# One product for two in the sums over features, and a weight remainder issued behind the norms' reciprocal

## The chip, the core and the metric

The kernel runs on one core of a Trainium2 chip. Its engines each work through a queue of their own: TensorE (PE, with its weight loads PEld), VectorE (DVE), ScalarE (ACT), GpSimd (POOL), and SyncE (SP), which issues the loads. The metric is the device time of one execution in microseconds; the kernel before takes 1084.68 us (median of 3 runs, 1083.91 to 1085.72).

## What is computed

Two layers of a hybrid decoder on 288 tokens (256 of a prompt, 32 of eight samples), 1024 features wide. Each layer has four token mixers with gates, an output product, a SwiGLU mixer and two LayerNorms; the Conformer mixer has a LayerNorm of its own over 256 channels. What the change touches are these norms:

```python
def layer_norm(x, g, b):
    xf = x.astype(jnp.float32)
    mu = jnp.mean(xf, -1, keepdims=True)
    var = jnp.mean(jnp.square(xf - mu), -1, keepdims=True)
    return ((xf - mu) * lax.rsqrt(var + LN_EPS) * g + b).astype(x.dtype)

    b_out = jax.nn.silu(layer_norm(cv + conv_b, conv_ln_g, conv_ln_b))
    ...
    x1 = layer_norm(ALPHA * x + merged @ w_o, ln1_g, ln1_b)
    ...
    r = r + (pe @ w_pe) * jax.nn.sigmoid(r @ w_pg)
    y = layer_norm(r, ln2_g, ln2_b)
```

## The kernel before

Features lie on the 128 partitions, tokens along the free axis: `xf` is 8 tiles of 128x288 in f32. Every matrix product with weights is three products of PE (L292 to L294, or L315, L321, L319 in `outer`): the rounded weight `whi` with the rounded input, `whi` with the input's remainder, and the weight's remainder `wlo` with the rounded input.

The weights come as 306 groups of 8 blocks of 128x128. `W` counts blocks; at each new group `fetch` issues what is due ahead: the load of a group (SP, `load`, tile `wraw`, 4 buffers), its rounding (ACT, `high`, L264, tile `whi`, 4 buffers) up to three groups ahead, and its remainder (DVE, `low`, L271, tile `wlo`, 3 buffers) up to two groups ahead. `fetch(g, 2)` issues only roundings that are due for group g, `fetch(g, 3)` only remainders. While `hold` is true, as in the last product ahead of a norm and in the norm itself, a new group issues loads alone.

A sum over features is a product with the constant `o1024` (every element 1/1024) in plain f32. The program writes one such instruction, and the trace shows two PE records for it.

**The two big norms of a layer** (`ln`, four calls in all). `ln_part` and `ln_square` have by then summed seven of the eight tiles: `lnt[:,1]` is the sum of tiles 4 to 6 (tiles 0 to 3 were centred earlier, in `ln_pivot`), `lnt[:,2]` is a sum of squares that POOL adds up, and `lnt[:,0]` the square of tile 7. `ln` issues the remainder that is due, then the first half of the mean product `mu` (L402), sixteen small products in quarters (`quarters`, L395) for the mean and the mean square of each token, and the second half of `mu` (L407). Then come the variance (ACT L411, DVE L412, ACT L415), a copy of `mu` to SBUF for POOL (ACT L417), one rounding (ACT L264, by `fetch(self.group - 1, 2)`), the reciprocal (DVE L419), and its spread over the partitions (PE L424, tile `rs`). After that DVE and POOL subtract the mean (L430, L432), and for each tile k, `first` multiplies with `rs` (DVE L437) and rounds with scale and offset (ACT L439, tile `xh`), `second` makes the remainder (DVE L446, L448, tile `xl`), and `after(k)` is PE's next weight product, which reads `xh` of tile k. So that PE has work meanwhile, `fill` puts small weight products with `w_pe` at three places: ahead of the sums, behind them, and behind the spread. The first norm of a layer has 4 blocks (12 products) at each of the places 1 and 2; the second norm of layer 0 has 2, 4 and 2 blocks; the last norm of all has none, and no weights are left by then. At tile 2 `fetch(self.group)` issues all that is due.

**The Conformer norm** (`conv`) is a generator that a planner steps once for each group of weights, so its instructions lie scattered among the gate products of the input projection. It sums the two tiles `cv[:,0]` and `cv[:,1]` with two products (L702), subtracts, squares on ACT (L708), and sums the two squares `sq` with two more (L712). Each `yield` of two numbers charges a cost to the planner for DVE and ACT.

Of the kernel before, what the change touches and what calls it, by code (L numbers as in the profile page):

```python
# [14 lines left out]
OP = mybir.AluOpType  # L15
# [99 lines left out]
class Builder:  # L115
# [268 lines left out]
    def ln(self, g, b, after=None, fill={}):  # L384

        nc, xf = self.nc, self.xf
        g, b = self.par(g), self.par(b)
        q = N // 4
        st, mu = self.ax(), self.ax()[:, :N]
        m4, s4 = st[:, :q], st[:, q:2 * q]  # L390
        o = self.c("o1024")

        def quarters(out, src, first=False, last=False):
            for j in range(4):
                nc.tensor.matmul(out[32 * j:32 * j + 32], o[:, :32], src[:, q * j:q * j + q], start=first, stop=last)  # L395

        d, d2, d7, d72 = self.lnt[:, 1], self.lnt[:, 2], xf[:, KD - 1], self.lnt[:, 0]
        self.fetch(self.group, 3)
        out = {}
        if 0 in fill:  # L400
            out[0] = fill[0]()
        nc.tensor.matmul(mu, o, d, start=True, stop=False)  # L402
        quarters(m4, d, first=True)
        quarters(m4, d7)
        quarters(s4, d2)
        quarters(s4, d72, last=True)
        nc.tensor.matmul(mu, o, d7, start=False, stop=True)  # L407
        if 1 in fill:
            out[1] = fill[1]()
        t = [self.sb.tile([128, q], F32, name="q", tag="q", bufs=3) for _ in range(3)]  # L410
        nc.scalar.activation(t[0], m4, AF.Square)  # L411
        nc.vector.tensor_tensor(t[1], s4, t[0], op=OP.subtract)  # L412
        if 0 in fill:
            out[0]()
        nc.scalar.activation(t[2], t[1], AF.Sqrt, bias=self.c("eps"))  # L415
        mus = self.lnt[:, 3]
        nc.scalar.activation(mus, mu, AF.Copy)  # L417
        self.fetch(self.group - 1, 2)
        nc.vector.reciprocal(t[1], t[2])  # L419
        if 1 in fill:  # L420
            out[1]()
        rs = self.ax()[:, :N]
        for j in range(4):
            nc.tensor.matmul(rs[:, q * j:q * j + q], self.c("ident")[:, 32 * j:32 * j + 1].to_broadcast([128, 128]),  # L424
                             t[1], start=True, stop=True)
        if 2 in fill:
            out[2] = fill[2]()
        nd = 2 if after else 3
        for k in range(nd):
            nc.vector.tensor_tensor(xf[:, k], xf[:, k], mu, op=OP.subtract)  # L430
        for k in range(nd, KD):
            nc.gpsimd.tensor_tensor(xf[:, k], xf[:, k], mus, op=OP.subtract)  # L432
        ys = {}

        def first(k):
            y = ys[k] = self.s()
            nc.vector.tensor_tensor(y, xf[:, k], rs, op=OP.mult)  # L437
            if after:
                nc.scalar.activation(self.xh[:, k], y, AF.Identity, bias=b[:, k:k + 1], scale=g[:, k:k + 1])  # L439

        def second(k):
            y = ys.pop(k)
            if not after and k not in (3, 7):
                nc.scalar.activation(xf[:, k], y, AF.Identity, bias=b[:, k:k + 1], scale=g[:, k:k + 1])
            else:
                nc.vector.tensor_scalar(xf[:, k], y, g[:, k:k + 1], b[:, k:k + 1], op0=OP.mult, op1=OP.add)  # L446
            if after:
                nc.vector.tensor_tensor(self.xl[:, k], xf[:, k], self.xh[:, k].bitcast(F32), op=OP.subtract)  # L448
            elif k in (0, 1, 3, 5, 6, 7):
                c = slice(k - 1 if k in (3, 5) else k, k + 1)  # L450
                nc.sync.dma_start(self.d["y"][:, c], xf[:, c])

        first(0)
        if 2 in fill:
            out[2]()
        second(0)
        first(1)
        for k in range(2, KD + 2):
            if k < KD:
                first(k)  # L460
            if k <= KD:
                second(k - 1)
            if k == 2:
                self.hold = False
                self.fetch(self.group)
            if after:
                after(k - 2)
                if k == 7:
                    self.ln_warm(AF.Sigmoid)
        self.free()  # L470
# [197 lines left out]
    def conv(self):  # L668
        nc = self.nc
        ce, w = self.ce, self.par("conv_w")  # L670
        cv = yield from self.get_b([128, 2, N])
        bias = self.par("conv_b")
        es = [ce[:, c, 30 + TP:].rearrange("p (b w) -> p b w", b=NB) for c in range(2)]
        yield VECTOR
        for j in range(31):
            for c in range(2):
                wj = w[:, 31 * c + j:31 * c + j + 1]
                o, e = cv[:, c, :TP], ce[:, c, j:j + TP]
                if j == 0:
                    nc.vector.tensor_scalar(o, e, wj, bias[:, c:c + 1], op0=OP.mult, op1=OP.add)  # L680
                else:
                    nc.vector.scalar_tensor_tensor(o, e, wj, o, op0=OP.mult, op1=OP.add)  # L682
                yield 0.49, 0
        pr = yield from self.get_b([128, NB, TS, 31])
        for c in range(2):
            e = es[c]
            e = bass.AP(tensor=e.tensor, offset=e.offset, ap=[list(e.ap[0]), [34, NB], [1, TS], [1, 31]])
            nc.vector.tensor_tensor(pr, e, w[:, None, None, 31 * c:31 * c + 31].to_broadcast([128, NB, TS, 31]),
                                    op=OP.mult)
            yield 1.1, 0  # L690
            nc.vector.tensor_reduce(bt(cv[:, c, TP:]), pr, axis=AX.X, op=OP.add)
            yield 1.1, 0
            nc.vector.tensor_scalar(cv[:, c, TP:], cv[:, c, TP:], bias[:, c:c + 1], None, op0=OP.add)
            yield 0.1, 0
        yield BOTH
        self.free()
        self.free()
        yield 1
        mu, var = yield from self.get_ax(2)
        mu, var = mu[:, :N], var[:, :N]  # L700
        for c in range(2):
            nc.tensor.matmul(mu, self.c("o1024"), cv[:, c], start=c == 0, stop=c == 1)  # L702
        sq = [self.s(), self.s()]
        for c in range(2):
            nc.vector.scalar_tensor_tensor(cv[:, c], mu, -4.0, cv[:, c], op0=OP.mult, op1=OP.add)
            yield 0.4, 0
        for c in range(2):
            nc.scalar.activation(sq[c], cv[:, c], AF.Square)  # L708
        yield 0, 0.8
        yield 1  # L710
        for c in range(2):
            nc.tensor.matmul(var, self.c("o1024"), sq[c], start=c == 0, stop=c == 1)  # L712
        sd = self.s()
        nc.scalar.activation(sd, var, AF.Sqrt, bias=self.c("eps"), scale=4.0)
        yield 0, 2.0
        yield 1
        self.free_ax(2)
        rs = self.s()
        nc.vector.reciprocal(rs, sd)
        yield 2.0, 0  # L720
        g, b = self.par("cg"), self.par("cb")
        t = [self.s(), self.s()]
        for c in range(2):
            nc.vector.tensor_tensor(cv[:, c], cv[:, c], rs, op=OP.mult)
            yield 0.4, 0
        for c in range(2):
            nc.vector.tensor_scalar(cv[:, c], cv[:, c], g[:, c:c + 1], b[:, c:c + 1], op0=OP.mult, op1=OP.add)
            yield 0.4, 0
        for c in range(2):
            nc.scalar.activation(t[c], cv[:, c], AF.Sigmoid)  # L730
            yield 0, 0.45
        yield 1
        for c in range(2):
            nc.vector.tensor_tensor(cv[:, c], cv[:, c], t[c], op=OP.mult)
            yield 0.4, 0
        self.br["conv"] = yield from self.parts(cv)
# [353 lines left out]
    def layer(self, l, outs):  # L1090
# [22 lines left out]
        self.pe_load(l)  # L1113
        self.branch(3, "attn", 4)
        self.finish(conv)
        self.drop_ax(self.tick + 1)
        assert not self.tasks and self.ax_live == 0 and self.b_live == 2 + l, (self.ax_live, self.b_live)
# [186 lines left out]
def bt(a):  # L1304
    return a.rearrange("p (b t) -> p b t", b=NB)
# [134 lines left out]
```

## Time and profile before

| | |
|---|---|
| device time, median of 3 runs | 1084.68 us |
| device time of the profiled execution | 1083.62 us |
| its span, first to last instruction | 1081.8 us |
| PE busy | 1066.2 us (99%) |
| PE weight loads busy | 1030.5 us (95%) |
| DVE busy | 770.9 us (71%) |
| ACT busy | 557.5 us (52%) |
| POOL busy | 174.4 us (16%) |
| mean granted clock of PE | 0.996 |

The profiled execution lasts 1.8 us longer than its span, and 1.1 us less than the median. PE's records overlap (a product of 288 columns has a record of 0.29 us and the next starts some 0.13 us later), so the distance of starts is what a product costs, and a stretch in which starts lie at that distance is PE-bound. A row of the timeline merges like instructions that follow each other; in square brackets stands how long the engine had been idle and what ended that.

### The profile page before, as it was taken

How to read it: one execution, taken by the hardware profiler on the slowest of the kernel's cores; microseconds unless marked ns; L12 is line 12 of the kernel's file. 1: busy time of each engine (PE TensorE's matmuls, PEld its weight loads, DVE VectorE, ACT ScalarE, POOL GpSimd, SP SyncE). 2: the span in 40 equal slices, each digit the busy share in tenths (PEclk: the TensorE clock that was granted, in tenths of full speed). 3: DMA queues.
4: the chain of work that ended last, by engine and by line, in shares of the span. 5: the costliest groups of instructions: out<-in, count | busy, mean ns of one | idle time of the engine just before them, and what ended most of it. 6: DMA issues, size and time to landing. Idle time of an engine off the chain costs nothing.

```text
span 1081.8 us, 20642 instructions
## 1 busy us (share of the span) xinstructions
PE 1066.2 (99%) x8138; PEld 1030.5 (95%) x8138; DVE 770.9 (71%) x1305; ACT 557.5 (52%) x930; POOL 174.4 (16%) x175
## 2 busy tenths in 40 slices
PE   9999999999999999999999999999999999999996
PEld 8999989999999999999999998899999999999995
DVE  5898858678785555545789897687698765555456
ACT  5866445455564444434578565363545644443334
POOL 0720003005500000000437100030055000000004
PEclk9999999999999999999999999999999999999998
DMA  9476566344445555554445856563453644554541
GB/s 320 153 260 205 180 238 212 115 163 150 153 156 176 156 172 169 166 160 166 167 151 176 283 175 211 195 212 119 152 168 118 196 159 163 173 171 159 173 137 44
DMA packets 61732, 188.58 MB, mean 174 GB/s; under 512 B 7587, under 2 KB 12227, under 8 KB 61635
## 3 DMA queue, kind: packets, MB, share of 16 engines
q1 hardware_dynamic: 60498, 183.54, 51.5%
q0 software_dynamic: 992, 3.57, 0.9%
q8 instruction: 64, 1.05, 0.4%
q14 instruction: 34, 0.27, 0.1%
q10 hardware_dynamic: 144, 0.15, 0.1%
HBM read 182.48 MB, written 4.75 MB: 173 GB/s over the span
## 4 chain that ended last, share of the span: by engine, by line
PE 91%; DVE 4%; ACT 2%; POOL 2%; issue 1%; DMA 0%; SPq 0%; DVEq 0%; POOLq 0%; ACTq 0%
PE mm L292 24%; PE mm L293 24%; PE mm L294 24%; PE mm L319 2%; PE mm L321 2%; PE mm L315 2%; DVE wlo L271 1%; PE ax L293 1%; PE ax L292 1%; PE ax L294 1%; PE ax L321 1%; POOL b L341 1%; PE ax L319 1%; PE ax L315 1%; POOL b L372 1%
## 5 line engine op out<-in xcount | busy, mean ns | idle before, releaser
L271 DVE TENSOR_TENSOR wlo<-wraw,whi 128x1024 fp32r<-128x1024 f32 (+1 forms) x309 | 384.4, 1246 | 144.6 <-issue 79.6
L292 PE MATMUL mm<-xh,whi 128*128 128x288 f32 x1536 | 455.3, 296 | 0.8 <-DVE s L1060 0.8
L294 PE MATMUL mm<-xh,wlo 128*128 128x288 f32 x1536 | 453.1, 295 | 0.9 <-DVE wlo L271 0.8
L293 PE MATMUL mm<-xl,whi 128*128 128x288 f32 x1536 | 453.2, 295 | 0.0
L264 ACT ACTIVATE whi<-wraw 128x1024 fp32r<-128x1024 f32 (+1 forms) x309 | 322.6, 1046 | 152.3 <-PE mm L293 80.7
L292 PEld LDWEIGHTS mm<-xh,whi 128*128 128x128 f32 x1536 | 288.8, 188 | 8.6 <-issue 7.4
L294 PEld LDWEIGHTS mm<-xh,wlo 128*128 128x128 f32 x1536 | 288.6, 188 | 1.7 <-DVE wlo L271 1.6
L293 PEld LDWEIGHTS mm<-xl,whi 128*128 128x128 f32 x1536 | 288.8, 188 | 0.4
L292 PE MATMUL mm<-b,whi 128*128 128x288 f32 x576 | 171.8, 298 | 0.0
L293 PE MATMUL mm<-b,whi 128*128 128x288 f32 x576 | 169.9, 295 | 0.0
L294 PE MATMUL mm<-b,wlo 128*128 128x288 f32 x576 | 169.5, 294 | 0.0
L292 PEld LDWEIGHTS mm<-b,whi 128*128 128x128 f32 x576 | 107.9, 187 | 0.9 <-issue 0.4
L294 PEld LDWEIGHTS mm<-b,wlo 128*128 128x128 f32 x576 | 108.5, 188 | 0.0
L293 PEld LDWEIGHTS mm<-b,whi 128*128 128x128 f32 x576 | 108.1, 188 | 0.3
L1061 POOL TENSOR_TENSOR m<-m,s 128x288 f32<-128x288 f32 x32 | 38.2, 1226 | 273.5 <-DVE s L1060 273.5
L339 POOL TENSOR_TENSOR b<-xf 128x288 f32<-128x288 f32 x4 | 4.9, 1220 | 443.5 <-DVE xf L1206 434.8
L1179 ACT ACTIVATE b<-s 128x288 fp32r<-128x288 f32 x44 | 19.3, 445 | 92.1 <-DVE s L1174 92.1
L682 DVE SCALAR_TENSOR_TENSOR b<-b,prm 128x256 f32<-128x256 f32 x120 | 63.1, 573 | 0.0
L1174 DVE TENSOR_TENSOR s<-s,mm 128x288 f32<-128x288 f32 x40 | 18.0, 454 | 50.4 <-PE mm L294 50.4
L1045 ACT ACTIVATE xf<-mm 128x288 f32<-128x288 f32 x32 | 13.2, 412 | 63.0 <-PE mm L294 63.0
L1045 ACT ACTIVATE g<-mm 128x288 f32<-128x288 f32 x32 | 13.2, 412 | 60.2 <-PE mm L294 60.1
L1182 DVE TENSOR_TENSOR b<-s,b 128x288 fp32r<-128x288 f32 x44 | 19.8, 458 | 19.4 <-ACT b L1179 19.4
(252 smaller groups left out, 1235.1 us busy)
## 6 DMA issues: line engine op xcount, KB each, us to landing
wraw<-in_w_dram SPq DMA_DIRECT2D x304, 512.0 KB, 3.5
kv<-in_ck_dram SPq DMA_DIRECT2D x32, 256.0 KB, 5.3
kv<-in_cv_dram SPq DMA_DIRECT2D x32, 256.0 KB, 4.8
out_ko_dram<-b POOLq DMA_DIRECT2D x2, 576.0 KB, 5.0
out_vo_dram<-b POOLq DMA_DIRECT2D x2, 576.0 KB, 7.2
kv<-in_kidx_dram SPq DMA_DIRECT2D x32, 32.0 KB, 3.1
b<-in_p_dram SPq DMA_DIRECT2D x3, 288.0 KB, 4.0
wraw<-in_w_dram SPq DMA_DIRECT2D x3, 256.0 KB, 4.8
```

The source lines that it names most:

```text
L264: self.nc.scalar.activation(self.hi[g][:, c[i]], self.raw[g][:, c[i]], AF.Copy)
L271: self.nc.vector.tensor_tensor(self.lo[g][:, c[i]], self.raw[g][:, c[i]], self.hi[g][:, c[i]].bitcast(F32), op=OP.subtract)
L292: m(out, wh, rh, start=first, stop=False)
L293: m(out, wh, rl, start=False, stop=False)
L294: m(out, wl, rh, start=False, stop=last)
L315: m(o, wh, rh[:, k], start=k == 0, stop=False)
L319: m(o, wh, rl[:, k], start=False, stop=not early and k == nk - 1)
L321: m(o, wl, rh[:, k], start=False, stop=False)
L682: nc.vector.scalar_tensor_tensor(o, e, wj, o, op0=OP.mult, op1=OP.add)
L1045: self.nc.scalar.activation(g, a, AF.Sigmoid)
L1061: nc.gpsimd.tensor_tensor(self.m[:, j], self.m[:, j], t, op=OP.add)
L1182: nc.vector.tensor_tensor(h[:, 1, i % 2], t, h[:, 0, i % 2].bitcast(F32), op=OP.subtract)
```

## The change

In `ln`, DVE adds the sum of tiles 4 to 6 and tile 7 into `lnt[:,3]`, and one product with that sum takes the place of the two halves of `mu`; it stands behind the fill at place 1. The call that issues due remainders moves from the head of `ln` to behind the reciprocal; the text of the call is the same, but `self.group` is read there later. In `conv`, DVE adds the two tiles ahead of the mean product and the two squares ahead of the other, and one product remains of each two.

```diff
@@ ln
         d, d2, d7, d72 = self.lnt[:, 1], self.lnt[:, 2], xf[:, KD - 1], self.lnt[:, 0]
-        self.fetch(self.group, 3)
+        nc.vector.tensor_tensor(self.lnt[:, 3], d, d7, op=OP.add)
         out = {}
         if 0 in fill:
             out[0] = fill[0]()
-        nc.tensor.matmul(mu, o, d, start=True, stop=False)
         quarters(m4, d, first=True)
         quarters(m4, d7)
         quarters(s4, d2)
         quarters(s4, d72, last=True)
-        nc.tensor.matmul(mu, o, d7, start=False, stop=True)
         if 1 in fill:
             out[1] = fill[1]()
+        nc.tensor.matmul(mu, o, self.lnt[:, 3], start=True, stop=True)
...
         nc.scalar.activation(mus, mu, AF.Copy)
         self.fetch(self.group - 1, 2)
         nc.vector.reciprocal(t[1], t[2])
+        self.fetch(self.group, 3)
         if 1 in fill:
             out[1]()
@@ conv
+        both = self.s()
+        nc.vector.tensor_tensor(both, cv[:, 0], cv[:, 1], op=OP.add)
+        yield 0.45, 0
...
-        for c in range(2):
-            nc.tensor.matmul(mu, self.c("o1024"), cv[:, c], start=c == 0, stop=c == 1)
+        nc.tensor.matmul(mu, self.c("o1024"), both, start=True, stop=True)
...
+        nc.vector.tensor_tensor(sq[0], sq[0], sq[1], op=OP.add)
+        yield 0.45, 0
         yield 1
-        for c in range(2):
-            nc.tensor.matmul(var, self.c("o1024"), sq[c], start=c == 0, stop=c == 1)
+        nc.tensor.matmul(var, self.c("o1024"), sq[0], start=True, stop=True)
```

What this does to the order, first on DVE, in the first norm of layer 0. `q` are the quarters' tiles, `b` the norm's sums, `ax_3701` to `ax_3754` PSUM tiles of the norm, `s` the products of `first`. Before, from the remainder at the head of `ln` on:

```order
L271 TENSOR_TENSOR wlo_3703<-wraw_3542,whi_3638 128x1024
L412 TENSOR_TENSOR q_3740<-ax_3701,q_3739 128x72
L419 RECIPROCAL q_3740<-q_3741 128x72
L430 TENSOR_TENSOR xf_69<-xf_69,ax_3702 128x288 x2
L437 TENSOR_TENSOR s_3778<-xf_69,ax_3751 128x288
L446 TENSOR_SCALAR xf_69<-s_3778,prm_218 128x288
L448 TENSOR_TENSOR xl_71<-xf_69,xh_70 128x288
L437 TENSOR_TENSOR s_3785<-xf_69,ax_3751 128x288
L437 TENSOR_TENSOR s_3788<-xf_69,ax_3751 128x288
L446 TENSOR_SCALAR xf_69<-s_3785,prm_218 128x288
L448 TENSOR_TENSOR xl_71<-xf_69,xh_70 128x288
L271 TENSOR_TENSOR wlo_3795<-wraw_3591,whi_3746 128x1024
```

The same place of the changed kernel:

```order
L398 TENSOR_TENSOR b_3535<-b_3535,xf_69 128x288
L411 TENSOR_TENSOR q_3739<-ax_3702,q_3738 128x72
L418 RECIPROCAL q_3739<-q_3740 128x72
L271 TENSOR_TENSOR wlo_3748<-wraw_3543,whi_3639 128x1024
L271 TENSOR_TENSOR wlo_3750<-wraw_3592,whi_3745 128x1024
L430 TENSOR_TENSOR xf_69<-xf_69,ax_3703 128x288 x2
L437 TENSOR_TENSOR s_3781<-xf_69,ax_3754 128x288
L446 TENSOR_SCALAR xf_69<-s_3781,prm_218 128x288
L448 TENSOR_TENSOR xl_71<-xf_69,xh_70 128x288
```

Two remainders stand behind the reciprocal now, since the fill at place 1 has gone on to the next group: the one from the head of `ln` and the one that was issued at tile 2. The same holds in the second norm of layer 0 and the first of layer 1; in the last norm no remainder is due.

ACT's order is that of before; in the changed kernel it reads, at the same place:

```order
L410 ACTIVATE q_3738<-ax_3702 128x72
L414 ACTIVATE q_3740<-q_3739,const0_213 128x72
L416 ACTIVATE b_3535<-ax_3703 128x288
L264 ACTIVATE whi_3745<-wraw_3592 128x1024
L1089 ACTIVATE m_3701<-mm_3721 128x288
L1089 ACTIVATE m_3701<-mm_3730 128x288
L439 ACTIVATE xh_70<-s_3781,prm_218 128x288
```

The rounding `whi_3745`, which the second of DVE's two remainders reads, stands behind the copy of `mu` (`ax_3703`), as its counterpart did before.

PE in the same norm, before:

```order
L402 MATMUL ax_3702<-b_3534,const0_213 128x288
L395 MATMUL ax_3701<-b_3534,const0_213 32x72 x4
L395 MATMUL ax_3701<-xf_69,const0_213 32x72 x4
L395 MATMUL ax_3701<-b_3534,const0_213 32x72 x8
L407 MATMUL ax_3702<-xf_69,const0_213 128x288
L292 MATMUL mm_3723<-b_3096,whi_3593 128x288
```

and the end of the fill at place 1 in the changed kernel, where the quarters are followed by the fill at once:

```order
L292 MATMUL mm_3730<-b_3097,whi_3594 128x288
L293 MATMUL mm_3730<-b_3097,whi_3594 128x288
L294 MATMUL mm_3730<-b_3097,wlo_3641 128x288
L408 MATMUL ax_3703<-b_3535,const0_213 128x288
L424 MATMUL ax_3754<-q_3739,const1_214 128x72 x4
```

The mean product has moved from around the quarters to between the fill and the spread of the reciprocal.

## Rows read from the trace of the kernel before

**Rows 1.** Page, the chain that ended last, shares of the span by engine.
```profile
PE 91%; DVE 4%; ACT 2%; POOL 2%; issue 1%; DMA 0%; SPq 0%; DVEq 0%; POOLq 0%; ACTq 0%
```

**Rows 2.** Timeline (start us, us, engine, line), PE, Conformer norm of layer 0, mean.
```profile
228.30 0.29 PE L294 MATMUL mm<-xh,wlo 128*128 128x288 f32 x1
228.43 1.13 PE L702 MATMUL ax<-b,const 128*128 128x288 f32 x4
...
229.53 0.29 PE L293 MATMUL mm<-xl,whi 128*128 128x288 f32 x1
```

**Rows 3.** Timeline, DVE, the same stretch.
```profile
228.68 1.23 DVE L271 TENSOR_TENSOR wlo<-wraw,whi 128x1024 fp32r<-128x1024 f32 x1 [1.79 <-issue]
```

**Rows 4.** Timeline, PE, first norm of layer 0, sums.
```profile
291.87 0.65 PE L402 MATMUL ax<-b,const 128*128 128x288 f32 x2
...
293.02 0.46 PE L395 MATMUL ax<-b,const 128*32 128x72 f32 x16
293.40 0.75 PE L407 MATMUL ax<-xf,const 128*128 128x288 f32 x2
293.78 0.51 PE L292 MATMUL mm<-b,whi 128*128 128x288 f32 x1
```

**Rows 5.** Timeline, PE, the same norm, spread and first product behind the norm.
```profile
295.59 1.00 PE L424 MATMUL ax<-q,const 128*128 128x72 f32 x8
...
298.08 0.43 PE L315 MATMUL mm<-xh,whi 128*128 128x288 f32 x2
```

**Rows 6.** Timeline, ACT, the same norm.
```profile
293.54 0.23 ACT L411 ACTIVATE q<-ax 128x72 f32<-128x72 f32 x1 [0.48 <-PE ax L395]
...
294.48 0.39 ACT L417 ACTIVATE b<-ax 128x288 f32<-128x288 f32 x1
294.77 1.05 ACT L264 ACTIVATE whi<-wraw 128x1024 fp32r<-128x1024 f32 x1
...
297.12 0.63 ACT L439 ACTIVATE xh<-s,prm 128x288 fp32r<-128x288 f32 x1 [0.70 <-DVE s L437]
```

**Rows 7.** Timeline, DVE, the same norm.
```profile
292.44 1.60 DVE L271 TENSOR_TENSOR wlo<-wraw,whi 128x1024 fp32r<-128x1024 f32 x1
...
295.13 0.75 DVE L430 TENSOR_TENSOR xf<-xf,ax 128x288 f32<-128x288 f32 x2
296.63 0.46 DVE L437 TENSOR_TENSOR s<-xf,ax 128x288 f32<-128x288 f32 x1 [0.75 <-PE ax L424]
```

**Rows 8.** Timeline, PE, second norm of layer 0.
```profile
536.56 0.75 PE L402 MATMUL ax<-b,const 128*128 128x288 f32 x2 [0.68 <-DVE b L378]
...
538.45 0.75 PE L407 MATMUL ax<-xf,const 128*128 128x288 f32 x2
...
542.85 0.54 PE L315 MATMUL mm<-xh,whi 128*128 128x288 f32 x2 [0.36 <-ACT xh L439]
```

**Rows 9.** Timeline, DVE, a remainder while POOL adds squares, layer 0.
```profile
288.60 1.83 DVE L271 TENSOR_TENSOR wlo<-wraw,whi 128x1024 fp32r<-128x1024 f32 x1
```

**Rows 10.** Timeline, POOL, the mean's subtraction in the first norm of layer 0.
```profile
294.95 4.91 POOL L432 TENSOR_TENSOR xf<-xf,b 128x288 f32<-128x288 f32 x6 [1.99 <-ACT b L417]
```

**Rows 11.** Timeline, PE, tiles 1 and 2 behind the second norm of layer 0.
```profile
546.43 0.42 PE L315 MATMUL ax<-xh,whi 128*128 128x288 f32 x2
546.93 0.53 PE L321 MATMUL mm<-xh,wlo 128*128 128x288 f32 x2
```

**Rows 12.** Timeline, PE, the last norm.
```profile
1073.16 1.16 PE L424 MATMUL ax<-q,const 128*128 128x72 f32 x8 [0.96 <-DVE q L419]
```

**Rows 13.** Window (us; PE, PEld, DVE, ACT, POOL busy; granted clock, DMA) behind the last spread.
```profile
1074.40:1075.40 1.00, 0.00 (x0) 0.00 (x0) 1.00 (x3) 0.55 (x2) 1.00 (x2) 0.50 0.00 0
```

**Rows 14.** Timeline, PE, the kernel's start.
```profile
0.79 3.22 PE L1238 MATMUL ax<-const-float32-0.0 128*128 128x288 f32 x6 [0.79 <-PEq L1347]
...
4.85 0.68 PE L319 MATMUL mm<-xl,whi 128*128 128x288 f32 x2
5.33 0.61 PE L321 MATMUL mm<-xh,wlo 128*128 128x288 f32 x2
```

## Prediction
> **What bounds the kernel now.** I read the page's chain first: PE holds 91% of the chain that ended last [rows 1], so nearly everywhere a microsecond of PE's stream is one of the span, and what other engines do costs only where PE waits for it. Then the timeline of PE around the sums that are edited, and of DVE, ACT and POOL beside it. In the Conformer norm PE streams without a wait: weight products 0.13 us apart, four records of the mean, weight products again [rows 2]. In the big norms it is a race: PE has its fills, and ACT and DVE have to bring xh of tile 0 before the fills run out. In the first norm of layer 0 xh ends at 297.12 + 0.63 = 297.75, and PE takes it at 298.08 [rows 5, 6]: a margin of 0.33 us. In the second norm there is none; PE waits 0.36 us for it [rows 8]. So whatever is put on that path beyond 0.33 us, PE waits out.
>
> **The Conformer sums.** From 228.30 to 229.53 [rows 2] are six steps, two of them of weight products; (1.23 - 0.26) / 4 = 0.24 us a record, so a product of two records is worth 0.48. Two of them go in each layer, four in all: **-1.9 us**, all on PE's stream. The additions that replace them go to DVE, some 0.5 us each. The one ahead of the mean falls where DVE then stands idle 1.79 us for the next group [rows 3]; the one of the squares waits for ACT in the same kind of gap. PE takes either sum only a group of weights later. Nothing for both; if the cover were gone, 0.5 each.
>
> **The big norms, products.** The first half of the mean is covered today: the quarters behind it wait for POOL, tile 7 and ACT, and in the second norm it only begins once DVE's L378 is through [rows 4, 8]. Without it PE waits longer in the same places: nothing. The second half (L407) is not saved: one product of the same size now runs behind the fill. So PE's own work there stays as it was (bounds: 0 to -0.5 a norm; I take 0, since all inputs of the quarters keep their times). In the last norm nothing is due and PE waits 0.96 us for the reciprocal anyway [rows 12]: 0.
>
> **The remainders.** The order shows two remainders of 1024 columns between the reciprocal and the subtraction in three of the four norms. The second of them reads a rounding that ACT makes behind the copy of the mean; and the mean is ready later now. I follow it in the first norm of layer 0. The quarters end as before, so the fill starts at 293.40 in L407's place. It has taken 295.59 - 293.78 = 1.81 us [rows 4, 5], so the mean product starts at 295.21, its second record 0.24 later; with a record of 0.41 it ends at 295.86. ACT follows 0.06 behind (293.02 + 0.46 to 293.54 [rows 4, 6]; I take this hop between any two engines): the copy starts at 295.92 instead of 294.48. The rounding starts 0.29 behind it and takes 1.05 [rows 6]: 297.26. DVE has made the first remainder meanwhile and stands waiting; it starts the second at 297.32.
>
> How long that takes is the open price. Alone a remainder takes 1.23 us [rows 3]; beside POOL's additions one took 1.83 [rows 9] and the one at the norm's head 1.60 [rows 7]. POOL's six subtractions, 4.91 us in a row, start when the copy of the mean is done [rows 10], so they run right then; I take 1.83, and 1.23 as the low end: 299.15. Then two subtractions (0.75 [rows 7]); of two instructions in a row the second starts some 0.1 before the end of the first (294.48 + 0.39 against 294.77 [rows 6]), which takes off 0.2: 299.70. From there L437 to L439 0.49, and 0.63 for xh [rows 6, 7]: 300.82, and PE at 300.88 instead of 298.08: **+2.8 us**. On the same distance, 7.48 us behind the start of the fill, the second norm comes to 538.45 + 7.48 = 545.93 instead of 542.85 [rows 8]: **+3.1**. The first norm of layer 1 has the same orders: +2.8. Together 8.7; without the share for POOL 6.9.
>
> The Trainium skill, "SBUF — State Buffer", section "Who interferes with whom", has a rule that speaks against this change: a DVE instruction with two inputs in SBUF and a GpSimd instruction that reads SBUF take turns, and the later one is blocked for the whole of the other. The trace agrees (1.23 alone, 1.83 beside POOL). By the rule at its worst, a whole subtraction of 4.91 / 6 = 0.82 us, each norm would be 0.2 longer, and the sum 0.7.
>
> Something is given back. The second remainder was due at tile 2, and there PE waited for it: two L321 follow two L315 by 0.50 us instead of 0.26 [rows 11]. I take 0.24 in each of the three: -0.7. The remainder taken from the head also frees the variance step, but that is ahead of the fill's end and is not what PE waits for. The loads on SP's queue that wait for a remainder's buffer leave some 2.6 us later once, and are read several groups later: nothing.
>
> Sum without the clock: -1.9 + 8.7 - 0.7 = **+6.0 us** (low end 4.2). The profiled execution's 1083.62 (span 1081.8 and 1.8 around it) would become 1089.6; the median 1084.68 stands 1.1 above it, and becomes 1090.7.
>
> **The clock.** PE would wait from about 298.18 (the spread starts 0.1 later) to 300.88, 2.7 us, and 3.3 in the second norm. The longest such wait in these rows is the 0.96 us of the last norm [rows 12], and just there the granted clock goes to 0.50, from 2.4 to 1.2 GHz [rows 13], although small products ran on either side of the wait. So I expect it to fall in waits three times as long. The price per norm: at the start, PE's products begin at 0.79, and as late as 4.85 to 5.33 two weight products still took 0.48 us [rows 14], 0.24 each instead of 0.13; if PE's work behind a norm ran like that for as long, some 4.6 us, it would lose 45% of it, 2.1 us; none if the clock holds. I take the middle, 1.05, three times: **+3.2 us**, between 0 and 6.3.
>
> The Trainium skill, "TensorE: Matmul & The Clock Gate", section "Why this matters for your kernels", warns that gaps between bursts bring the half clock back; the row of the last norm is of that kind, no row here shows how soon full speed returns in mid-kernel.
>
> **The rivals.**
> (A) DVE's second remainder holds up xh, and the clock falls: 1084.7 + 6.0 + 3.2 = 1093.9. For it: the order, and rows 13. Its own range is 1088.9 (no POOL share, no fall) to 1097.0 (6.3 for the clock).
> (B) The same without a fall: 1090.7. For it: PE is dense up to the wait and behind it, which the last norm isn't.
> (C) Faster: both remainders are through before PE has ended the spread, since nothing but the product's place has moved ACT. Then xh comes as before, and with PE's stream the bound each of three norms gains its product too: -1.9 - 3 x 0.48, which is 1081.3. It decides at 296.7, the end of the spread (295.69 + 1.0); my sum has the second remainder end at 299.15, and its input alone at 297.26.
> (D) The delay is there but the fills cover it, so that the Conformer's 1.9 us alone shows: 1082.8. Against it: a margin of 0.33 us in one norm, and none in another. That the change doesn't do what it says holds in part already: of eight products it takes away, four were covered.
>
> **How the numbers follow.** A 0.57, B 0.28, C 0.04, D 0.05, and 0.06 for more than A's end. Forecast 1093.9, the likeliest. The range reaches from B's low side to A's end, 1088.5 to 1097.3, and leaves out C, D and the rest, 0.15. A measurement of this kernel can tell about 0.2%, 2.2 us, from no change: A, B and the rest are slower by more (0.91), D is within it (0.05), C is faster (0.04).
>
> **What would show it.** L702 and L712 have two records instead of four in a layer, with no wait ahead of them. In three norms DVE stands idle about 1 us ahead of the second of two L271, ended by ACT's L264; xh of tile 0 comes some 7.5 us behind the start of the fill, and PE's first L315 has an idle time of some 2.5 to 3.3 us ahead of it, ended by ACT's L439. The clock's part shows as a window of half clock behind a norm. I would be wrong if the first L315 had no such wait, if the remainder took no longer beside POOL (then -1.8), or if the half clock lasted much longer than the start's.

## The result, and the profile after

The changed kernel takes 1095.22 us (median of 4 runs, 1093.03 to 1097.76) against 1084.51 us of the kernel before (4 runs): a ratio of 1.0098, 95% interval 1.0073 to 1.0123. It is slower by 10.7 us; 1093.9 was forecast, within 1088.5 to 1097.3. The profiled execution took 1094.42 us, with a mean granted clock of 0.991 (0.996 before).

From the page of the changed kernel: its span, the busy times, the chain that ended last (before: [rows 1]), and one group, with busy time and mean ns, then the idle time ahead of it and what ended most of that.

```profile
span 1092.7 us, 20622 instructions
...
PE 1066.6 (98%) x8122; PEld 1032.6 (95%) x8122; DVE 774.5 (71%) x1313; ACT 558.6 (51%) x930; POOL 177.1 (16%) x175
...
PE 89%; DVE 4%; ACT 3%; POOL 2%; issue 1%; DMA 1%; SPq 0%; POOLq 0%; DVEq 0%; ACTq 0%
...
L315 PE MATMUL mm<-xh,whi 128*128 128x288 f32 x128 | 27.4, 310 | 8.7 <-ACT xh L439 8.3
```

PE is busy for 0.4 us more than before, although it has 16 records fewer (8122 for 8138); the last line says where most of the 10.9 us come from by which the span is longer: ahead of L315 PE idles 8.7 us, 8.3 of them for ACT's xh. That is the wait behind three norms.

The Conformer sums did what was forecast. PE's timeline (start us, us, engine, line, operation, idle time before in brackets) at the place of [rows 2]:

```profile
228.89 0.29 PE L294 MATMUL mm<-xh,wlo 128*128 128x288 f32 x1
229.02 0.65 PE L704 MATMUL ax<-s,const 128*128 128x288 f32 x2
229.29 0.51 PE L292 MATMUL mm<-xh,whi 128*128 128x288 f32 x1
229.63 0.29 PE L293 MATMUL mm<-xl,whi 128*128 128x288 f32 x1
```

From L294 to L293 are 0.74 us where it was 1.23: 0.49 saved by one product, without a wait. DVE's addition (L696, 227.51, 0.46 us) lies in the gap of [rows 3].

Then the first norm of layer 0: PE, as in [rows 4, 5].

```profile
292.62 0.46 PE L395 MATMUL ax<-b,const 128*32 128x72 f32 x16
293.01 0.40 PE L292 MATMUL mm<-b,whi 128*128 128x288 f32 x1
...
294.71 0.65 PE L408 MATMUL ax<-b,const 128*128 128x288 f32 x2
295.20 1.01 PE L424 MATMUL ax<-q,const 128*128 128x72 f32 x8
...
300.35 0.99 PE L315 MATMUL mm<-xh,whi 128*128 128x288 f32 x4 [2.51 <-ACT xh L439]
```

And what it waits for, DVE and ACT in the same norm, as in [rows 6, 7]:

```profile
294.59 1.16 DVE L271 TENSOR_TENSOR wlo<-wraw,whi 128x1024 fp32r<-128x1024 f32 x1
296.79 1.76 DVE L271 TENSOR_TENSOR wlo<-wraw,whi 128x1024 fp32r<-128x1024 f32 x1 [1.04 <-ACT whi L264]
298.47 0.81 DVE L430 TENSOR_TENSOR xf<-xf,ax 128x288 f32<-128x288 f32 x2
299.20 0.44 DVE L437 TENSOR_TENSOR s<-xf,ax 128x288 f32<-128x288 f32 x1
```

```profile
295.40 0.41 ACT L416 ACTIVATE b<-ax 128x288 f32<-128x288 f32 x1 [1.36 <-PE ax L408]
295.70 1.05 ACT L264 ACTIVATE whi<-wraw 128x1024 fp32r<-128x1024 f32 x1
...
299.67 0.63 ACT L439 ACTIVATE xh<-s,prm 128x288 fp32r<-128x288 f32 x1 [2.32 <-DVE s L437]
```

It reads as a chain: the mean product ends at 295.36, ACT copies it and only then rounds; DVE has made its first remainder and stands 1.04 us for that rounding; the second remainder takes 1.76 us, since POOL's subtractions run from 295.88; xh ends at 300.30 and PE goes on at 300.35. Before it was 298.08, on a stream that stood 0.39 later (293.40 against 293.01).

What came behind the wait: windows (PE, PEld, DVE, ACT, POOL busy with instructions in brackets, granted clock, DMA share, GB/s) of the changed kernel behind its three norms,

```profile
301.60:304.90 3.30, 3.30 (x16) 3.30 (x15) 2.30 (x5) 2.93 (x4) 0.15 (x1) 0.50 0.00 0
305.00:308.30 3.30, 3.30 (x27) 3.30 (x27) 3.16 (x7) 2.21 (x3) 0.00 (x0) 1.00 0.49 170
...
550.80:554.10 3.30, 3.30 (x16) 3.30 (x15) 2.30 (x5) 2.75 (x4) 0.00 (x0) 0.50 0.00 0
...
840.90:844.20 3.30, 3.19 (x13) 3.19 (x14) 2.27 (x5) 2.72 (x7) 1.49 (x2) 0.50 0.32 122
```

and of the kernel before in the first of these stretches:

```profile
301.60:304.90 3.30, 3.30 (x26) 3.14 (x25) 3.27 (x6) 2.45 (x4) 0.00 (x0) 1.00 0.52 169
```

From its first product on PE is full in all of them (in the third stretch that is at 841.01), but at clock 0.50 (1.2 GHz instead of 2.4) it starts 13 to 16 products where at 1.00 it starts 26 or 27.

Laying PE's products of the two profiled executions side by side, the 10.9 us of span are: +0.6 at 32 us, where PE waits 1.00 us for a weight remainder instead of 0.44, ahead of anything that the change touches; four times -0.49 in the Conformer norms; +3.95, +3.9 and +3.8 in the three norms; +0.7 in the last norm. There the half clock came behind the spread of the reciprocal in the kernel before [rows 12, 13], and comes ahead of it now, so that its eight records start 0.21 us apart instead of 0.11. The spread and a window around it in the changed kernel:

```profile
1083.38 1.98 PE L424 MATMUL ax<-q,const 128*128 128x72 f32 x8 [0.96 <-DVE q L418]
```

```profile
1083.20:1085.00 1.80, 1.62 (x8) 1.62 (x8) 1.16 (x4) 0.00 (x0) 1.80 (x3) 0.50 0.00 0
```

Each of the three norms' parts splits into the later xh (+2.64, +2.94, +2.75), the half clock (+1.5, +1.5, +1.2) and what tile 2 gives back (-0.2, -0.56, -0.2).

### The profile page after: what moved, and what is told of

It reads as the page before. It is cut to its first block, busy times and chain, and to the rows that moved or that the text cites. A ratio compares the mean times of both kernels' runs of the same rounds, so it can differ in the third digit from the quotient of the medians.

```text
span 1092.7 us, 20622 instructions
## 1 busy us (share of the span) xinstructions
PE 1066.6 (98%) x8122; PEld 1032.6 (95%) x8122; DVE 774.5 (71%) x1313; ACT 558.6 (51%) x930; POOL 177.1 (16%) x175
## 4 chain that ended last, share of the span: by engine, by line
PE 89%; DVE 4%; ACT 3%; POOL 2%; issue 1%; DMA 1%; SPq 0%; POOLq 0%; DVEq 0%; ACTq 0%
PE mm L292 24%; PE mm L293 24%; PE mm L294 24%; PE mm L315 2%; PE mm L321 2%; PE mm L319 2%; DVE wlo L271 2%; DMA wraw<-in_w_dram 1%; ACT whi L264 1%; PE ax L321 1%; PE ax L293 1%; PE ax L294 1%; PE ax L292 1%; POOL b L341 1%; PE ax L319 1%
## 5 line engine op out<-in xcount | busy, mean ns | idle before, releaser
L292 PE MATMUL mm<-xh,whi 128*128 128x288 f32 x1536 | 455.4, 296 | 0.9 <-DVE s L1063 0.9
L294 PE MATMUL mm<-xh,wlo 128*128 128x288 f32 x1536 | 453.1, 295 | 1.4 <-DVE wlo L271 1.4
L293 PE MATMUL mm<-xl,whi 128*128 128x288 f32 x1536 | 453.2, 295 | 0.0
L294 PEld LDWEIGHTS mm<-xh,wlo 128*128 128x128 f32 x1536 | 288.7, 188 | 2.3 <-DVE wlo L271 2.1
L293 PEld LDWEIGHTS mm<-xl,whi 128*128 128x128 f32 x1536 | 288.8, 188 | 0.4
L293 PE MATMUL mm<-b,whi 128*128 128x288 f32 x576 | 169.9, 295 | 0.0
L294 PE MATMUL mm<-b,wlo 128*128 128x288 f32 x576 | 169.5, 294 | 0.0
L294 PEld LDWEIGHTS mm<-b,wlo 128*128 128x128 f32 x576 | 108.4, 188 | 0.0
L293 PEld LDWEIGHTS mm<-b,whi 128*128 128x128 f32 x576 | 108.1, 188 | 0.1
L315 PE MATMUL mm<-xh,whi 128*128 128x288 f32 x128 | 27.4, 310 | 8.7 <-ACT xh L439 8.3
```

The source lines that it names most:

```text
L292: m(out, wh, rh, start=first, stop=False)
L293: m(out, wh, rl, start=False, stop=False)
L294: m(out, wl, rh, start=False, stop=last)
L315: m(o, wh, rh[:, k], start=k == 0, stop=False)
```

## The experiments

All ratios are to the kernel before, run on the same chip (1084.14 to 1084.36 us there).

| kernel | us (lowest to highest) | ratio | 95% |
|---|---|---|---|
| changed kernel again (e0) | 1095.39 (1094.13 to 1097.43) | 1.0101 | 1.0084 to 1.0118 |
| Conformer part alone (e1) | 1082.64 (1081.62 to 1083.30) | 0.9982 | 0.9974 to 0.9991 |
| the same again, beside e8 and e9 | 1082.94 (1081.93 to 1083.65) | 0.9985 | 0.9976 to 0.9994 |
| big norms' part alone (e2) | 1094.50 (1093.56 to 1095.44) | 1.0092 | 1.0077 to 1.0107 |
| one remainder moved, not two (e3) | 1086.58 (1084.99 to 1087.53) | 1.0018 | 1.0010 to 1.0027 |
| mean product ahead of the fill (e4) | 1089.55 (1088.43 to 1093.25) | 1.0063 | 1.0043 to 1.0082 |
| rounding ahead of the copy (e5) | 1086.66 (1086.30 to 1088.32) | 1.0025 | 1.0013 to 1.0037 |
| PE kept busy in the wait (e6) | 1090.25 (1089.86 to 1091.52) | 1.0061 | 1.0044 to 1.0077 |
| sum as one product, all else kept (e7) | 1083.69 (1082.58 to 1084.22) | 0.9993 | 0.9984 to 1.0002 |
| e7 with an unread product in L402's place (e8) | 1083.08 (1082.36 to 1084.28) | 0.9991 | 0.9982 to 1.0000 |
| e3 with the same (e9) | 1085.20 (1084.30 to 1085.70) | 1.0009 | 1.0000 to 1.0018 |

**The two parts, each alone.** e1 has the `conv` part of the diff and the old `ln`, e2 the reverse. The theory: the Conformer part is a gain, the norms' part is the loss, and the two add up.

> The Conformer norm's part of the change alone; the big norms as before. Theory (PE streams there, a product of two records is worth 0.48 us, the additions are covered): four products less, -1.9 us, 1082.6 us. Rival (the additions or their planner costs move something else): not below 1084. The trace should show L702's successor with two records and the same distance of starts to either side.

> The big norms' part of the change alone; the Conformer norm as before. Theory: the whole loss is here and the two parts add up: 1084.5 + 10.7 + 1.9 = 1097.1 us, with three half-clock stretches behind the norms. Rival (the Conformer part adds to the loss): below 1096.

e1 gave 1082.64, 1.7 us under the kernel before: the Conformer's four products and nothing else. So the gain is real, and it is the best of all kernels here. e2 fell 2.6 us short of its number. That is under the 1096 of the rival, but not for the rival's reason, since e1 alone is faster. Its profiled execution shows a part of it: the waits are there in all three norms (2.51, 3.30 and 2.51 us; 2.51, 3.30 and 2.52 in the changed kernel), but behind the third the clock held. First a window of e2 behind its second norm, then one around the third, with PE's timeline there:

```profile
550.80:554.10 3.30, 3.30 (x17) 3.30 (x16) 2.31 (x6) 2.75 (x4) 0.81 (x1) 0.55 0.08 34
842.00:845.30 3.30, 2.62 (x18) 2.51 (x19) 2.71 (x6) 2.71 (x6) 2.07 (x3) 1.00 0.41 153
```

```profile
842.68 0.99 PE L315 MATMUL mm<-xh,whi 128*128 128x288 f32 x4 [2.51 <-ACT xh L439]
```

It is the same length of wait ahead of the same product that was followed by half clock in the first norm of the changed kernel, and in its third (2.52 us, at 841.01). So the parts add up in waits, but the clock's part is a matter of the single execution; the mean clocks of e2's four executions (0.992 to 0.994) lie above nearly all of the changed kernel's eight (0.986 to 0.993). Why the clock held more often in e2 is open.

**The change once more.** Nothing is edited; it stands beside e4 to e6 on one chip.

> The changed kernel once more, beside the three that follow on the same chip: about 1095 us, with a wait of 2.5, 3.3 and 2.5 us for xh in three norms and a half-clock stretch behind each.

The result repeats: 1.0101. In its profiled execution, the slowest of its four (1097.43 us, clock 0.986), half clock came at 300.9, 550.1 and 843.6 us, in the norms' waits for xh, and besides at 34.7, behind a wait of 1.9 us for a weight remainder, and at 543.2, early in the second norm's fill. Falls like these two can set runs of one kernel 3 us apart.

**Is the clock a cost of its own?** Against e0, e6 puts unread products into PE's wait, five in the first norm of a layer and six in the second. If the theory holds, xh stays late and only the clock is given back; the rival is that PE was slow for another reason, the weights, say.

```diff
@@ outer, where it takes its accumulators
+                for _ in range(self.idle):
+                    self.nc.tensor.matmul(outs[0], self.c("o1024"), self.c("cos"), start=True, stop=True)
+                self.idle = 0
@@ ahead of the two calls of ln
+        self.idle = 5
...
+            self.idle = 6
```

> As the changed kernel, with 5, 6 and 5 products that nobody reads (the constant with a constant, into the bank that the next product clears) put into PE's wait for xh in the three norms; they end before xh comes. Theory (the wait costs twice: itself, and the clock that falls in it): xh at the same place, the granted clock stays at 1.00 behind the norms, 1.5 us less in each, about 1090.7 us. Rival (the clock falls for another reason, or the slow products behind the norm come from elsewhere): no gain, 1095 us.

PE's timeline of e6 in the first norm, and the window behind it:

```profile
297.82 2.59 PE L311 MATMUL mm<-const 128*128 128x288 f32 x10
300.50 0.99 PE L319 MATMUL mm<-xh,whi 128*128 128x288 f32 x4
```

```profile
302.30:305.60 3.30, 3.30 (x27) 3.30 (x27) 2.30 (x5) 2.59 (x4) 0.00 (x0) 1.00 0.00 0
```

The first product with xh starts at 300.50, as late as before (300.35), but the clock holds: 27 products in 3.3 us instead of 16. That is worth 5.1 us (1095.39 to 1090.25). What is left over e1, 7.6 us, is the late xh itself, with its give-back 2.4 us of PE's stream in each norm of the profiled executions, and the last norm's spread, which for the most part ran at half clock in e6 as well (0.65 us). That last part stands in the profiled executions of the changed kernel, e0, e2 to e6 and e9, and in none of the others; why is open.

**Is it the second remainder?** e5 swaps two lines of ACT, so that the rounding is not queued behind the copy of the mean:

```diff
-        nc.scalar.activation(mus, mu, AF.Copy)
         self.fetch(self.group - 1, 2)
+        nc.scalar.activation(mus, mu, AF.Copy)
```

> As the changed kernel, but ACT makes the rounding ahead of the copy of the mean, so the second remainder's input is ready when the first is done; both remainders still stand behind the reciprocal. Theory (DVE waits about 1 us for that rounding, and then 0.6 for POOL, which would start only after DVE here): xh 1.7 us earlier, PE waits some 0.8 us, the clock holds, about 1085.5 us. Rival (two remainders in the queue are what costs, whenever their inputs come): as the changed kernel, 1095 us.

DVE of e5 in the first norm, with PE's first product behind it:

```profile
295.21 2.29 DVE L271 TENSOR_TENSOR wlo<-wraw,whi 128x1024 fp32r<-128x1024 f32 x2
297.42 0.81 DVE L430 TENSOR_TENSOR xf<-xf,ax 128x288 f32<-128x288 f32 x2
```

```profile
299.31 1.00 PE L315 MATMUL mm<-xh,whi 128*128 128x288 f32 x4 [0.85 <-ACT xh L439]
```

The wait of 1.04 us between the remainders is gone, and both together take 2.29 us although POOL's subtractions start at 296.50, while the second remainder runs. Here it is POOL that waits. Its first subtraction in e5, and below it the second and the third in the changed kernel:

```profile
296.50 1.68 POOL L432 TENSOR_TENSOR xf<-xf,b 128x288 f32<-128x288 f32 x1 [3.31 <-ACT b L417]
```

```profile
296.65 0.81 POOL L432 TENSOR_TENSOR xf<-xf,b 128x288 f32<-128x288 f32 x1
297.42 1.78 POOL L432 TENSOR_TENSOR xf<-xf,b 128x288 f32<-128x288 f32 x1
```

So what counts is which of the two starts first: in e5 the remainder does and POOL's subtraction takes 1.68 us; in the changed kernel the remainder starts at 296.79, 0.14 us into a subtraction of 0.81, and takes 0.60 us longer, and then POOL's next takes 1.78. PE waits 0.85 us here (1.64 and 0.84 in the other two norms) and keeps its clock. Two swapped lines give 8.7 of the change's 11.2 us back, the clock's part with them. e4 takes another way to the same wait: it puts the mean product ahead of the fill, so that ACT has the mean early.

```diff
+        nc.tensor.matmul(mu, o, self.lnt[:, 3], start=True, stop=True)
         if 1 in fill:
             out[1] = fill[1]()
-        nc.tensor.matmul(mu, o, self.lnt[:, 3], start=True, stop=True)
```

> As the changed kernel, but the mean product stands ahead of the fill, where its second half stood before; the copy of the mean and the rounding are some 1.4 us earlier, and so are POOL's subtractions. Theory (beside POOL a remainder takes 0.6 us longer): DVE waits for nothing, but now both remainders run beside POOL, 1.8 us each, and xh comes only some 0.45 us earlier; PE waits about 2 us; 1093.8 us if the clock still falls, 1089.3 if it holds. Rival (the wait for the rounding is all that matters, POOL costs nothing): xh 1.0 to 1.7 us earlier, 1092 or less with falls.

DVE, POOL and PE of e4 there:

```profile
294.47 3.46 DVE L271 TENSOR_TENSOR wlo<-wraw,whi 128x1024 fp32r<-128x1024 f32 x2
```

```profile
294.29 6.84 POOL L432 TENSOR_TENSOR xf<-xf,b 128x288 f32<-128x288 f32 x6 [1.84 <-ACT b L416]
```

```profile
299.73 1.00 PE L315 MATMUL mm<-xh,whi 128*128 128x288 f32 x4 [2.01 <-ACT xh L439]
```

With the mean early DVE doesn't wait for the rounding either, but now POOL starts at 294.29 and both remainders run beside it: 3.46 us instead of e5's 2.29. Its three waits (2.01, 2.81, 2.02 us) add up to 6.8 us, and in this profiled execution the clock held behind each; it is the fastest of four (1088.43 us, mean clock 0.996), 5.8 us over e1. Two others ran at mean clocks of 0.993 and 0.991 and took 1090.21 and 1093.25 us, so the clock fell more in them. The copy's place costs by two ways, the queue on ACT and the start of POOL, and the two pull against each other.

**One remainder instead of two.** e3 issues behind the reciprocal only what was due at the head of `ln`:

```diff
-        self.fetch(self.group, 3)
+        self.fetch(self.group - 1, 3)
```

> As the changed kernel, but the call behind the reciprocal is for the group before, so that only the remainder from the head of the norm moves there and the other stays at tile 2. Theory (what costs is the second remainder, whose rounding stands behind the copy of the late mean): xh of tile 0 comes at most 0.3 us later than before, no long wait of PE, no half clock, about 1083 us. Rival (any remainder between reciprocal and subtraction holds xh up by its own 1.2 us): 1.2 x 3 on top of the Conformer's -1.9, about 1086 us.

My number was missed by 3.6 us, and the rival's was met, though not for its reason. xh of tile 0 is in time in the first norm: PE's first L315 is at 298.20 (e1: 298.07); in the second norm PE waits 0.87 us for it (e1: 0.36). DVE of e3 in the first norm from the reciprocal on shows what is late:

```profile
294.35 0.60 DVE L418 RECIPROCAL q<-q 128x72 f32<-128x72 f32 x1 [0.42 <-ACT q L414]
294.87 1.16 DVE L271 TENSOR_TENSOR wlo<-wraw,whi 128x1024 fp32r<-128x1024 f32 x1
...
299.55 0.96 DVE L446 TENSOR_SCALAR xf<-s,prm 128x288 f32<-128x288 f32 x1
300.61 0.88 DVE L448 TENSOR_TENSOR xl<-xf,xh 128x288 fp32r<-128x288 f32 x1
301.42 2.35 DVE L271 TENSOR_TENSOR wlo<-wraw,whi 128x1024 fp32r<-128x1024 f32 x2
303.69 0.44 DVE L437 TENSOR_TENSOR s<-xf,ax 128x288 f32<-128x288 f32 x1
```

and e1 at both ends of that stretch:

```profile
294.61 0.60 DVE L419 RECIPROCAL q<-q 128x72 f32<-128x72 f32 x1 [0.42 <-ACT q L415]
...
303.04 0.45 DVE L437 TENSOR_TENSOR s<-xf,ax 128x288 f32<-128x288 f32 x1
```

From the reciprocal to tile 2's L437 DVE takes 9.34 us instead of 8.43. The remainder puts L430 1.24 us further behind the reciprocal; only 0.76 of that lies where DVE in e1 waits for the spread (as in [rows 7]). And DVE's instructions for tiles 0 and 1 take 0.43 us more from one start to the next: POOL's subtractions run 1.2 us later and meet those of tile 1 (L446 0.96 and L448 0.88, in e1 0.42 and 0.46), while less of them is left over tile 0 (0.58 and 0.72, in e1 1.12 and 0.87). PE is 0.62 us later at tile 2 (303.84 against 303.22). At the head of `ln` the remainder had lain almost wholly in idle time.

**What the covered product was for.** A second thing in e3: half clock ahead of the second norm's fill. It is in e7 too. e7 leaves the remainder at the head, behind the addition, and the one mean product in L407's place, so that only the covered first half is gone:

```diff
@@ against the changed kernel
         nc.vector.tensor_tensor(self.lnt[:, 3], d, d7, op=OP.add)
+        self.fetch(self.group, 3)
...
         quarters(s4, d72, last=True)
+        nc.tensor.matmul(mu, o, self.lnt[:, 3], start=True, stop=True)
         if 1 in fill:
             out[1] = fill[1]()
-        nc.tensor.matmul(mu, o, self.lnt[:, 3], start=True, stop=True)
...
         nc.vector.reciprocal(t[1], t[2])
-        self.fetch(self.group, 3)
```

> The whole change but for two places: in the big norms the one mean product stands where the second half stood (ahead of the fill), and the remainder stays at the head of the norm, behind the new addition. Theory (the first half of the mean product was covered by waits for POOL, tile 7 and ACT, so removing it gives nothing): as the Conformer part alone, 1082.6 us. Rival (each removed product is worth its 0.48 us in the norms too): 1081.2 us.

It came out 1.05 us above e1 on the same chip. PE of e7 in the second norm, and the windows of the sums and of the fill:

```profile
535.98 0.33 PE L395 MATMUL ax<-b,const 128*32 128x72 f32 x8 [0.66 <-DVE b L378]
536.84 0.33 PE L395 MATMUL ax<-xf,const 128*32 128x72 f32 x8 [0.53 <-DVE xf L1209]
...
537.61 0.33 PE L395 MATMUL ax<-b,const 128*32 128x72 f32 x8 [0.31 <-ACT b L374]
```

```profile
535.30:538.40 3.10, 1.60 (x36) 1.08 (x35) 3.03 (x6) 2.62 (x7) 1.28 (x3) 0.99 0.65 209
538.40:541.70 3.30, 3.30 (x15) 3.16 (x15) 1.43 (x5) 2.18 (x6) 2.38 (x4) 0.50 0.45 159
```

No wait is longer than 0.66 us, but with the quarters alone between them PE is busy for only 1.60 of 3.10 us, and then the clock is at half through the fill. So I put the product back, as one whose sum nothing reads, in L402's place: e8 is e7 with it, e9 is e3 with it.

```diff
+        nc.tensor.matmul(mu, o, d, start=True, stop=True)
         quarters(m4, d, first=True)
```

> As e7_sum_only (one mean product in the place of the second half, the remainder at the head), with a product that nobody reads put where the first half stood; the next product into its bank clears it. Theory (the removed half cost nothing by itself, but it kept PE at work between two waits ahead of the quarters of the second norm, and without it the granted clock falls there in some executions): the clock holds at 1.00 through that norm, and the time is that of the Conformer part alone, 1082.6 us. Rival (what e7 lost against the Conformer part comes from DVE, whose addition stands ahead of the remainder and of the variance step): as e7, 1083.7 us.

> As e3_one_remainder, with the same unread product where the first half of the mean stood. Theory (e3 lost 4 us against the Conformer part: some 1.4 of it by the clock in the second norm, the rest because the subtractions and tiles 0 to 3 come later on DVE): the clock holds, 1085.4 us or a little less. Rival (all of e3's loss is the clock's): 1083 us.

> The Conformer part alone, once more, on the chip of the two others, to compare them with: 1082.6 us, no half clock before the end.

The same stretches in e8, whose stream is 0.84 us later there; then the window of the second norm's fill in e9, and below it in e3:

```profile
536.14:539.24 3.10, 2.12 (x38) 1.37 (x37) 3.03 (x6) 2.62 (x7) 1.28 (x3) 1.00 0.59 204
539.24:542.54 3.30, 3.30 (x27) 3.22 (x26) 1.99 (x7) 2.45 (x7) 2.38 (x4) 1.00 0.42 159
```

```profile
539.00:542.30 3.30, 3.30 (x26) 3.19 (x26) 2.60 (x5) 1.95 (x5) 0.64 (x1) 1.00 0.00 0
```

```profile
539.00:542.30 3.30, 3.30 (x21) 3.10 (x18) 1.91 (x3) 0.89 (x3) 0.00 (x0) 0.50 0.00 0
```

With one more product PE is busy for 2.12 of 3.10 us, and the clock is 1.00 through the fill. e8 lies 0.14 us from e1 where e7 lay 1.05, although DVE's addition, the rival, stands in e8 as in e7; e9 lies 1.4 us under e3, on another chip (1.25 by their distances to the kernel before). The profiled executions by themselves are few: half clock came at this fill in three of the eight without a product in that place (e0, e3 and e7; not in the changed kernel's other one, nor in e2, e4, e5 and e6), and in none of the five with one. The mean clocks of all executions point the same way: 0.995 in seven of e7's eleven, but 0.996 or 0.997 in each of e1's, e1 again's and e8's; 0.994 or 0.995 in eleven of e3's twelve, but 0.996 or 0.997 in ten of e9's eleven. So the cause is well supported. Its price in e7, some 0.6 to 0.9 us, isn't measured closely, since the intervals of e7 and e8 overlap. What e9 still has over e1 (2.3 us) lies in the three norms (0.74, 0.86 and 0.75 us of PE's stream in the profiled executions), where DVE's stretch is longer.

## Why the prediction was right, step by step

**The Conformer sums: right.** -1.9 forecast; four times -0.49 in the profile, -1.7 us (e1) and -1.3 (e1 again, 1082.94 against 1084.23) in the medians.

**The remainders and the late xh: right in each link, and in size.** From the start of the fill to PE's first L315 I had 7.48 us, and 7.34 were measured; 0.11 of the difference is the fill (1.70 us for 1.81). The second remainder was priced at 1.83 us and took 1.76; alone the first took 1.16. The delays were +2.64, +2.94 and +2.75 instead of +2.8, +3.1 and +2.8, in sum 8.3 for 8.7. e5 shows that it is this chain: with the rounding ahead of the copy, 8.7 us go, the clock's part among them.

The rule of the Trainium skill, "SBUF — State Buffer", section "Who interferes with whom", speaks of turns between DVE and GpSimd. The traces agree in kind: 1.16 alone and 1.76 beside POOL, and for two 2.29 where they start ahead of POOL and 3.46 where POOL starts ahead of them (e5, e4). The worst case that I drew from it, a whole subtraction of 0.82 us lost by each, was not reached: 0.60 and, in the mean of e4's two, 0.59. In the changed kernel the remainder came 0.14 us after the subtraction that it waited for, so nearly all of that one was still ahead.

**The give-back at tile 2: right in kind, a little small.** 0.2, 0.56 and 0.2 instead of three times 0.24.

**The clock: the mechanism was right, the term too small.** It fell behind all three norms in the profiled execution, at 1.5, 1.5 and 1.2 us, 4.2 for the 3.2 that I took as the middle between none and 6.3. That the middle came so close is luck in part: each fall was cheaper than the 2.1 us that I priced from the start, and all three came. By medians, e6 puts the term at 5.1, which has in it what fell elsewhere in e0's executions. The rows that I leaned on carried less than I read from them: in the kernel before, the spread behind the wait of 0.96 us still ran at full clock, eight records in 1.16 us [rows 12], and the half clock came only behind it [rows 13]. The changed kernel's clock term, 0.6 us at the start and 0.7 in the last norm, for which I had 0, put the forecast of 1093.9 below the 1095.2 measured; the xh and the give-back, both somewhat better than forecast, take 0.6 off again. The range's ends lie 0.4 and 0.3 us outside A's own (1088.9 and 1097.0), for which the text gives no reason; nothing hangs on that. Rival B, no fall, is e6's 1090.25 for the 1090.7 of the text: it would have been right had PE had work in the wait.

**"Nothing" for the covered half of the mean: failed in the reason.** It cost PE no time, as I said; I had not asked what else it did. It kept PE busy between the quarters' waits, and without it the clock can fall at the fill (e3, e7, and the profiled execution of e0). In the profiled execution of the changed kernel it didn't fall there, so the sum was not hurt.

**Rival C (both remainders in time) and D (the fills cover it)** fall with the 2.51 us of wait ahead of L315. e3 adds to it that even one remainder behind the reciprocal is not free.

What stays open is why the clock fell behind one wait of 2.51 us and not behind another; no run here varies that by itself.

## What to carry to other kernels

Count an instruction that is moved with all that its call issues at the new place: here a call with the same text issued two remainders, and the second stood behind a copy on another engine's queue. Before an operation off the critical path is removed or moved, ask what its place gave: the remainder filled DVE's idle time, and the covered product, as far as these runs go, kept PE's clock up. Where a change makes PE wait for microseconds, price the products behind the wait at either clock.

## What was not expected of the hardware

The half clock came without a long wait: in e7 behind idle times of 0.66, 0.53 and 0.31 us with only the small products of the quarters between them, and it held through a fill in which PE was full (3.30 of 3.30 us busy at 0.50). Nor did the wait's length alone decide it: behind waits of 2.51, 3.30 and 2.52 us it fell in the changed kernel, and behind the first two of e2's 2.51, 3.30 and 2.51 us, but it held behind the third; behind the 2.01, 2.81 and 2.02 us of e4's profiled execution it held. The Trainium skill, "TensorE: Matmul & The Clock Gate", section "HAM oscillation — how this bites in real kernels", tells of PE falling back to half rate in each wait for data; the traces agree that it happens in mid-kernel, but here it was in some executions and not in others of the same stretch.
